# Nine small edits to a one-core transformer-block kernel: the order of the down projection, four squares moved to another engine, a smaller sum of squares, later loads, one split matmul, and two banks for the last rows

## The chip, the cores and the metric

The kernel runs on one core of a Trainium2 chip. The metric is the device time of one execution in microseconds (us). Matmuls run on TensorE (PE, its weight loads PEld), element-wise work on VectorE (DVE), ScalarE (ACT) and GpSimd (POOL). SyncE (SP) issues most of the DMA transfers; POOL issues a few.

## The reference

One layer, 512 tokens, model width 1024, all in float32. Three sub-layers, each normalised before and after and added to the stream `x`:

```python
# 1. token mixer: heads 0-7 forgetting attention ("fox"), heads 8-15 chunked attention with relative bias
proj = rms_norm(x, g_mix_pre) @ w_in
o_fox, o_chk = fox_attention(...), chunked_rel_attention(...)           # 512 x 512 each
y = concat(rms_norm(o_fox, g_fox_out), rms_norm(o_chk, g_chunk_out)) @ w_out
x = x + rms_norm(y, g_mix_post)
# 2. cross-attention, 4 heads of 256, into 256 memory rows
q, (k, v) = rms_norm(x, g_mem_pre) @ w_mem_q, split(rms_norm(mem, g_mem_kv) @ w_mem_kv)
x = x + rms_norm(softmax(q k^T / 16) v @ w_mem_o, g_mem_post)
# 3. feed-forward, hidden width 2816
g, u = split(rms_norm(x, g_ffn_pre) @ w_gate_up)
x = x + rms_norm((silu(g) * u) @ w_down, g_ffn_post)
```

## The kernel before

**Precision.** Every product of two float32 matrices is three matmuls in a reduced type: each operand is split in a high part and a low rest, and `mm3` (line 142) adds high by high (L143), high by low (L144) and low by high (L146). With `parts=IN_STEP` (L140) it issues the last of the three as two matmuls of 128 columns instead of one of 256.

**Weights** come in 512 KB pieces. For the mixer and the cross-attention, `load_unit` (L106) loads a piece into `raw` (three buffers, issued by SP), ACT casts the high half (L125), DVE subtracts for the low half (L126). For the feed-forward network, pieces `fraw` go through a ring of slots: ACT casts `ring_hi` (L920), DVE subtracts `ring_lo` (L921). `take` (L1020) hands out slots in the order of a list of items and refills each slot that is free again.

**Mixer.** While `x` and the V weights stream in at the start, the squares of `x` are added up in `xs` (two blocks of 512 columns); `feature_rstd` (L251, called at L341) sums them over the features by fp32 matmuls with one column, four row tiles by two blocks. `head` (L523) works through four query tiles: scores, exponential, normalisation `p*rc` on DVE (L548), transposes on PE (L551), casts of the transposed `p` (ACT L553, DVE L554), products with V into bank `ps_o` (L560), ACT copy `ot` (L568) and a DVE add that gives the output pair `o` (L569). After each pair, `pair_out` (L571) makes its high and low halves (ACT, DVE) and has POOL square it (L577 the first of a group, L579 the others) and add the squares up (L580). `mem_norm` (L592) normalises the memory `mm` on DVE (L595) and splits it in `mT` (ACT L598, DVE L599).

**Order of instructions.** A tile scheduler sets the order on each engine from the order of the code and from priorities (`later`, L96), so that an instruction more or less in the attention moves its neighbours on other engines too.

**Mixer's end.** The first half of the output projection (fox heads) is mixed into the chunk heads. Then `kT` is made from `mT` and the K weights in four steps `c` (L694 is ACT's cast, L695 DVE's rest), POOL issues four loads `xo` of rows of `x` (L700), and the second half of the output projection follows, whose rows are finished with `xo` at L723.

**Feed-forward network.** The hidden width is cut in eleven blocks `u`. In most, gate and up are made by a seven-product scheme (`seven` L1108, products of 256 columns by `product` L1086); `IN_STEP` is asked for at `u` 1, 2, 4, 6 and 8 (L1186). The down projection (L1236 to the end) runs over the two halves of the output columns:

```python
SEVEN = (4, 5, 6, 7, 8)
DOWN = ((0, 1, 2, 3, 4, 5, 6, 7, 8, 9, 10), (0, 4, 5, 6, 7, 8, 1, 2, 3, 9, 10))
for half, tail in enumerate((2, 3)):
    body = DOWN[half][: FB // 2 - tail]
```

Blocks in `SEVEN` are done by seven products of 128 rows by 256 columns (`seven_products` L1276, using banks `p1 p5 p7 p6`), the others by 24 matmuls of 512 columns (`down` L1257: four row tiles, two k, three terms). After the last seven, `gather` (L1287) puts the seven-product sums together into `yd` on ACT and DVE. The last `tail` blocks are done row tile by row tile, and each row tile is finished (DVE add L1339/1348, ACT square, DVE gain L1341/1350) while the next one is multiplied. In half 1 the last row tile's tail is done in two halves of 256 columns, `left` and `right`, of one bank; then come the add, the square, the sum of squares, its power -0.5 on POOL (L1352), two DVE operations (L1355) and two output DMAs. `mm` (L1245) splits the third matmul of a product where `cuts` holds a column. While block 4 runs in half 0, the operands of blocks 9 and 8 are prepared (`late` L1226, `late_seven` L1207).

## Time and profile before

| what | before |
|---|---|
| median of 3 runs (lowest to highest) | 773.94 us (773.6 to 775.16) |
| the profiled execution | 775.14 us, its span 773.4 us |
| granted TensorE clock | 0.999 of full speed |
| PE busy | 758.1 us (98%), 5019 matmuls |
| DVE busy | 598.6 us (77%) |
| ACT busy | 429.3 us (56%) |
| POOL busy | 61.7 us (8%) |

The profiled execution took 1.2 us more than the median of the runs; 1.74 us of its time lie outside its span. Busy times are sums over the span. On PE a row's duration is longer than its distance to the next row, because matmuls overlap: the cost of a matmul on a full PE is the distance of starts. A bracket such as "[0.64 <-DVE p L548]" says that the engine stood idle 0.64 us before the row, and which instruction's end released it.

### The profile page before, as it was taken

How to read it: one execution, taken by the hardware profiler on the slowest of the kernel's cores; microseconds unless marked ns; L12 is line 12 of the kernel's file. 1: busy time of each engine (PE TensorE's matmuls, PEld its weight loads, DVE VectorE, ACT ScalarE, POOL GpSimd, SP SyncE). 2: the span in 40 equal slices, each digit the busy share in tenths (PEclk: the TensorE clock that was granted, in tenths of full speed). 3: DMA queues.
4: the chain of work that ended last, by engine and by line, in shares of the span. 5: the costliest groups of instructions: out<-in, count | busy, mean ns of one | idle time of the engine just before them, and what ended most of it. 6: DMA issues, size and time to landing. Idle time of an engine off the chain costs nothing.

```text
span 773.4 us, 12904 instructions
## 1 busy us (share of the span) xinstructions
PE 758.1 (98%) x5019; PEld 679.0 (88%) x5019; DVE 598.6 (77%) x1094; ACT 429.3 (56%) x782; POOL 61.7 (8%) x101
## 2 busy tenths in 40 slices
PE   9999999999999999999999999999999999999996
PEld 9977888887788888877778899999999999898985
DVE  8568889789886588554662779999899999987735
ACT  7468889667875457444563625554444445553421
POOL 1001132110321101000001100000000000000001
PEclk9999999999999999999999999999999999999999
DMA  7422113422323725321351202332433332333212
GB/s 272 119 76 81 28 56 87 132 82 63 109 75 105 274 85 189 120 70 57 109 158 33 82 29 82 111 110 82 138 110 109 109 108 87 107 106 113 102 62 109
DMA packets 60748, 80.05 MB, mean 104 GB/s; under 512 B 2704, under 2 KB 43664, under 8 KB 60688
## 3 DMA queue, kind: packets, MB, share of 16 engines
q1 hardware_dynamic: 59264, 74.49, 30.1%
q0 software_dynamic: 1280, 4.72, 1.8%
q8 instruction: 39, 0.64, 0.3%
q14 instruction: 21, 0.17, 0.1%
q10 hardware_dynamic: 144, 0.02, 0.0%
HBM read 77.13 MB, written 2.10 MB: 102 GB/s over the span
## 4 chain that ended last, share of the span: by engine, by line
PE 86%; ACT 6%; DVE 4%; issue 2%; DMA 2%; POOL 0%; DVEq 0%; POOLq 0%; ACTq 0%
PE ps_a L144 13%; PE ps_a L146 13%; PE ps_a L143 13%; PE ps_a L1090 3%; PE ps_a L1093 3%; PE ps_a L1091 3%; PE ps_s L1090 3%; PE ps_s L1091 3%; PE ps_s L1093 3%; PE ps_s L143 2%; PE ps_s L144 2%; PE ps_s L146 2%; PE ps_t L551 2%; DMA raw<-in_dram 2%; PE ps_o L560 2%
## 5 line engine op out<-in xcount | busy, mean ns | idle before, releaser
L920 ACT CAST ring_hi<-fraw 128x1024 fp32r<-128x1024 f32 (+1 forms) x62 | 57.3, 932 | 58.4 <-DVE fraw L999 17.5
L126 DVE TENSOR_TENSOR lo<-raw,hi 128x1024 fp32r<-128x1024 f32 x56 | 68.2, 1224 | 22.0 <-ACT hi L125 21.7
L921 DVE TENSOR_TENSOR ring_lo<-fraw,ring_hi 128x1024 fp32r<-128x1024 f32 (+1 forms) x62 | 66.4, 1074 | 17.2 <-ACT ring_hi L920 17.0
L146 PE MATMUL ps_a<-hTh,lo 128*128 128x512 f32 x192 | 76.7, 399 | 0.0
L144 PE MATMUL ps_a<-hTl,hi 128*128 128x512 f32 x192 | 75.9, 396 | 0.0
L143 PE MATMUL ps_a<-hTh,hi 128*128 128x512 f32 x192 | 75.9, 395 | 0.0
L125 ACT CAST hi<-raw 128x1024 fp32r<-128x1024 f32 x56 | 57.8, 1048 | 26.2 <-PE ps_a L144 18.3
L920 ACT CAST ring_hi<-sums 128x1024 fp32r<-128x1024 f32 x34 | 35.7, 1049 | 33.7 <-PE ps_t L1091 10.1
L921 DVE TENSOR_TENSOR ring_lo<-sums,ring_hi 128x1024 fp32r<-128x1024 f32 x34 | 41.4, 1218 | 2.1 <-ACT ring_hi L920 2.1
L144 PEld LDWEIGHTS ps_a<-hTl,hi 128*128 128x128 f32 x192 | 36.1, 188 | 6.4
L146 PEld LDWEIGHTS ps_a<-hTh,lo 128*128 128x128 f32 x192 | 36.1, 188 | 6.3
L143 PEld LDWEIGHTS ps_a<-hTh,hi 128*128 128x128 f32 x192 | 36.2, 188 | 5.7
L546 ACT ACTIVATE p<-p,nm 128x128 f32<-128x128 f32 (+1 forms) x64 | 36.1, 564 | 8.1 <-DVE nm L536 7.2
L1090 PE MATMUL ps_a<-b,ring_hi 128*128 128x256 f32 x140 | 39.1, 279 | 0.0
L1093 PE MATMUL ps_a<-b,ring_lo 128*128 128x256 f32 (+1 forms) x145 | 39.0, 275 | 0.0
L1091 PE MATMUL ps_a<-b,ring_hi 128*128 128x256 f32 x140 | 38.7, 277 | 0.0
L1090 PE MATMUL ps_s<-b,ring_hi 128*128 128x256 f32 x128 | 35.4, 276 | 0.0
L1091 PE MATMUL ps_s<-b,ring_hi 128*128 128x256 f32 x128 | 35.4, 276 | 0.0
L1093 PE MATMUL ps_s<-b,ring_lo 128*128 128x256 f32 x128 | 35.4, 276 | 0.0
L553 ACT CAST pth<-ps_t 128x128 fp32r<-128x128 f32 (+1 forms) x64 | 27.0, 425 | 14.5 <-PE ps_t L551 13.7
L554 DVE TENSOR_TENSOR ptl<-ps_t,pth 128x128 fp32r<-128x128 f32 (+1 forms) x64 | 30.7, 486 | 5.0 <-ACT pth L553 3.8
L551 PE MATMUL ps_t<-ident,p 128*128 128x128 f32 x160 | 28.1, 275 | 1.1 <-DVE p L548 0.8
(543 smaller groups left out, 2630.9 us busy)
## 6 DMA issues: line engine op xcount, KB each, us to landing
raw<-in_dram SPq DMA_DIRECT2D x64, 512.0 KB, 3.7
fraw<-in_dram SPq DMA_DIRECT2D x62, 512.0 KB, 3.5
cb<-in_dram SPq DMA_DIRECT2D x8, 256.0 KB, 2.9
xo<-in_dram POOLq DMA_DIRECT2D x4, 512.0 KB, 5.3
out_dram<-yd SPq DMA_DIRECT2D x8, 256.0 KB, 2.0
rawv<-in_dram SPq DMA_DIRECT2D x3, 520.0 KB, 6.6
xt<-in_dram SPq DMA_DIRECT2D x3, 512.0 KB, 6.7
gb<-in_dram POOLq DMA_DIRECT2D x3, 512.0 KB, 4.7
```

The costliest lines, as they stand in the source:

```text
L125: act.copy(hi[:, j : j + n, :], raw)
L126: dve.tensor_tensor(out=lo[:, j : j + n, :], in0=raw, in1=f32(hi[:, j : j + n, :]), op=ALU.subtract)
L143: pe.matmul(dst, sh, mh, start=first, stop=False)
L144: pe.matmul(dst, sh, ml, start=False, stop=False)
L146: pe.matmul(dst[:, to], sl, mh[:, to], start=False, stop=last)
L546: act.activation(p[:, :n], p[:, :n], AF.Exp, bias=nm, scale=-1.0, accum_out=sm)
L551: pe.transpose(tp[:, k * P : (k + 1) * P], p[:, k * P : (k + 1) * P], ident)
L920: act.copy(h2, v)
L921: dve.tensor_tensor(out=l2, in0=v, in1=f32(h2), op=ALU.subtract)
L1090: pe.matmul(dst, w[0][:, k, :], b[:, 0, k, :], start=first and k == 0, stop=False)
L1091: pe.matmul(dst, w[0][:, k, :], b[:, 1, k, :], start=False, stop=False)
L1093: pe.matmul(dst[:, to], w[1][:, k, :], b[:, 0, k, to], start=False, stop=last and k == 3)
```

## The change

Nine edits, in the order of the program (line numbers of the kernel before, with the changed kernel's in brackets where they differ):

1. The two blocks of `xs` are added by DVE (new L338), and `feature_rstd` sums one block.
2. `pair_out` gets `side`: squares of the chunk heads (side 1) are done by ACT instead of POOL; POOL still adds them up.
3. The four `xo` loads are issued after step 2 of the `kT` loop instead of after the loop, each buffer being written first by a POOL copy of a column of `kT` (new L705), which the load must then wait for.
4. Block 10 of gate and up asks for `IN_STEP` too.
5. In half 0 of the down projection block 10 stands between sevens 7 and 8, and the tail is one block, not two.
6. In half 0 the last seven gets a cut of a matmul like the first.
7. The preparation of blocks 9 and 8 is written after seven 6 instead of after seven 4.
8. The last row tile of half 1 is finished from two banks of its own, half by half: the sum of the body is added to `yd` before, each half is added, squared and multiplied by the gain alone.
9. The end of a row tile is a function, `finish_rows`.

```diff
             if k == 6:
                 add_squares(0, 4)
+                dve.tensor_tensor(out=xs[:, 0, :], in0=xs[:, 0, :], in1=xs[:, 1, :], op=ALU.add)
...
-                    rcol = feature_rstd(xs, range(2), NT, "rx")
+                    rcol = feature_rstd(xs, range(1), NT, "rx")
...
-        def pair_out(o, gc, oh, ol, sq, first, total):
+        def pair_out(o, gc, oh, ol, sq, first, total, side):
...
-            if first:
-                pool.tensor_tensor(out=sq, in0=o, in1=o, op=ALU.mult)
+            dst = sq if first else o
+            if side:
+                act.activation(dst, o, AF.Square)
             else:
-                pool.tensor_tensor(out=o, in0=o, in1=o, op=ALU.mult)
+                pool.tensor_tensor(out=dst, in0=o, in1=o, op=ALU.mult)
+            if not first:
                 pool.tensor_tensor(out=total, in0=sq, in1=o, op=ALU.add)
...
-        for t in range(NT):
-            nc.gpsimd.dma_start(xo[t], x[t * P : (t + 1) * P, :])
+                if c == 2:
+
+                    for t in range(NT):
+                        pool.tensor_copy(xo[t][:, :1], f32(kT[:, 0, 4, t : t + 1]))
+                        nc.gpsimd.dma_start(xo[t], x[t * P : (t + 1) * P, :])
...
-        DOWN = ((0, 1, 2, 3, 4, 5, 6, 7, 8, 9, 10), (0, 4, 5, 6, 7, 8, 1, 2, 3, 9, 10))
+        DOWN = ((0, 1, 2, 3, 4, 5, 6, 7, 10, 8, 9), (0, 4, 5, 6, 7, 8, 1, 2, 3, 9, 10))
...
-            parts = IN_STEP if u in (1, 2, 4, 6, 8) else WHOLE
+            parts = IN_STEP if u in (1, 2, 4, 6, 8, 10) else WHOLE
...
-        for half, tail in enumerate((2, 3)):
+        for half, tail in enumerate((1, 3)):
...
-                    if half == 0 and i == SEVEN[0]:
+                    if half == 0 and i in (SEVEN[0], SEVEN[-1]):
                         cuts.append(P)
                     seven_products(i, i == SEVEN[-1])
-                    if half == 0 and i == SEVEN[0]:
+                    if half == 0 and i == SEVEN[2]:
...
             for t in range(NT):
-                parts = (left, right) if half and t == NT - 1 else (slice(0, 512),)
                 yt = yd[:, t, cs]
...
+                if half and t == NT - 1:
+
+                    ss1, r = small(2, "fss2"), small(1, "frs")
+                    dve.tensor_tensor(out=yt, in0=accs[t], in1=yt, op=ALU.add)
+                    for n, (to, b) in enumerate(((left, bank("a")), (right, bank("a")))):
+                        for j, w in enumerate(ends):
+                            down(t, DOWN[half][FB // 2 - tail + j], w, j == tail - 1, (to,), b)
+                        dve.tensor_tensor(out=yt[:, to], in0=b[:, to], in1=yt[:, to], op=ALU.add)
+                        act.activation(junk3[:, to], yt[:, to], AF.Square, scale=1.0 / 32.0, accum_out=ss1[:, n : n + 1])
+                        if n == 0:
+                            dve.tensor_tensor(out=r, in0=ss1[:, :1], in1=ss0[:, t : t + 1], op=ALU.add)
+                        dve.tensor_tensor(out=gained[:, to], in0=yt[:, to], in1=gb3[:, c0 + to.start : c0 + to.stop], op=ALU.mult)
+                    dve.tensor_tensor(out=r, in0=ss1[:, 1:], in1=r, op=ALU.add)
+                    finish_rows(t, r)
+                    continue
```

**Order on ACT, at the end of the chunk heads.** `ps_o` is the bank of the last head's product with V, `ot` its copy, `mT` the memory's high half, `hi` the weights, `mix` the output projection's first half. Before:

```order
L553 CAST pth_413<-ps_t_2808 128x3x128
L553 CAST pth_413<-ps_t_2825 128x4x128
L656 ACTIVATE mix<-ps_a_2953,rsg_1877 128x512
L598 CAST mT<-mm 128x2048
L568 COPY ot_2841<-ps_o_2832 64x512
L125 CAST hi_3007<-raw_0_3009 128x1024
L125 CAST hi_3007<-raw_4_3013 128x1024
L656 ACTIVATE mix<-ps_a_2967,rsg_1877 128x512
L572 ACTIVATE oh<-o_2660,gn 128x512
```

And with the change:

```order
L554 CAST pth_410<-ps_t_2805 128x3x128
L554 CAST pth_410<-ps_t_2822 128x4x128
L659 ACTIVATE mix<-ps_a_2950,rsg_1874 128x512
L569 COPY ot_2838<-ps_o_2829 64x512
L601 CAST mT<-mm 128x2048
L573 ACTIVATE oh<-o_2657,gn 128x512
L125 CAST hi_3004<-raw_0_3006 128x1024
L125 CAST hi_3004<-raw_4_3010 128x1024
L659 ACTIVATE mix<-ps_a_2964,rsg_1874 128x512
L579 ACTIVATE o_2657<-o_2657 128x512
```

The copy `ot` now stands ahead of the cast of `mT`, the copy `oh` ahead of the two casts `hi`, and the new square (L579) comes last. On PE, 10 matmuls of the output projection now stand between the last product with V and the first matmul that reads `mT`, where there were 7.

**Order on POOL, from the second chunk pair to the loads of `xo`.** Before:

```order
L580 TENSOR_TENSOR sq_1869<-sq_1869,o_2046 128x512
L619 TENSOR_TENSOR msq<-msq 128x512 x3
L579 TENSOR_TENSOR o_2493<-o_2493 128x512
L151 TENSOR_TENSOR rm_2747<-rm_2747,mhalf 128x2
L580 TENSOR_TENSOR sq_1869<-sq_1869,o_2493 128x512
L579 TENSOR_TENSOR o_2660<-o_2660 128x512
L580 TENSOR_TENSOR sq_1869<-sq_1869,o_2660 128x512
L679 DMA gb<-in_dram 128x1024
L151 TENSOR_TENSOR rsg_2988<-rsg_2988,mhalf 128x4
L700 DMA xo_3003<-in_dram 128x1024
```

And with the change:

```order
L583 TENSOR_TENSOR sq_1866<-sq_1866,o_2043 128x512
L622 TENSOR_TENSOR msq<-msq 128x512 x3
L583 TENSOR_TENSOR sq_1866<-sq_1866,o_2490 128x512
L151 TENSOR_TENSOR rm_2744<-rm_2744,mhalf 128x2
L583 TENSOR_TENSOR sq_1866<-sq_1866,o_2657 128x512
L682 DMA gb<-in_dram 128x1024
L151 TENSOR_TENSOR rsg_2985<-rsg_2985,mhalf 128x4
L705 COPY xo_3000<-kT 128x1
L705 COPY xo_3001<-kT 128x1
L705 COPY xo_3002<-kT 128x1
L705 COPY xo_3003<-kT 128x1
L706 DMA xo_3000<-in_dram 128x1024
```

The squares have left POOL, the sums of them have stayed, and ahead of the first load of `xo` stand four copies that read `kT`.

## Rows read from the trace of the kernel before

**Rows 1.** The page: busy time of each engine, its share of the span and its instructions.

```profile
PE 758.1 (98%) x5019; PEld 679.0 (88%) x5019; DVE 598.6 (77%) x1094; ACT 429.3 (56%) x782; POOL 61.7 (8%) x101
```

**Rows 2.** Two windows of the span, the end of the chunk heads and the down projection: start and end, length, then busy us (and instructions) of PE, PEld, DVE, ACT and POOL, the granted PE clock, the busy share of the DMA engines and GB/s.

```profile
200.00:238.00 38.00, 37.74 (x202) 30.33 (x201) 31.64 (x90) 30.87 (x65) 7.89 (x6) 1.00 0.17 56
...
653.00:766.00 113.00, 113.00 (x727) 102.40 (x725) 85.73 (x137) 44.30 (x66) 2.21 (x4) 1.00 0.29 99
```

**Rows 3.** Timeline of the start, PE and DVE: the one-column matmuls of `feature_rstd` (L255), the next matmul, and the DVE operation behind them. Columns: start, duration, engine, line, operation, output<-input, shapes, count.

```profile
26.39 1.84 PE L255 MATMUL ps_t<-ones,xs 128*128 128x1 f32 x16
28.09 0.37 PE L143 MATMUL ps_s<-vhi,hTh 128*128 128x264 f32 x1
...
28.27 0.16 DVE L150 TENSOR_SCALAR rx<-ps_t 128x4 f32<-128x4 f32 x1 [5.85 <-PE ps_t L255]
```

**Rows 4.** Timeline of POOL, DVE and PE at two squares of the chunk pairs.

```profile
178.41 1.04 POOL L577 TENSOR_TENSOR sq<-o 128x512 f32<-128x512 f32 x1 [4.55 <-DVE o L569]
178.71 1.03 DVE L548 TENSOR_SCALAR p<-p,rc 128x512 f32<-128x512 f32 x1
179.35 0.40 PE L144 MATMUL ps_a<-hTl,hi 128*128 128x512 f32 x1
179.88 0.30 PE L551 MATMUL ps_t<-ident,p 128*128 128x128 f32 x1
...
197.47 1.03 POOL L579 TENSOR_TENSOR o<-o 128x512 f32<-128x512 f32 x1 [2.48 <-DVE rc L547]
197.69 0.89 DVE L548 TENSOR_SCALAR p<-p,rc 128x128 f32<-128x128 f32 x1
198.64 0.33 PE L551 MATMUL ps_t<-ident,p 128*128 128x128 f32 x1 [0.64 <-DVE p L548]
```

**Rows 5.** The lines L548, L617 (ACT's squares of the memory, 512 columns) and L580 (POOL's sums of squares) as groups: for the first two count, then least, median and longest ns; for the third count, busy us, mean ns and idle before.

```profile
L548 DVE TENSOR_SCALAR p<-p,rc x64: 270/410/1026, 63.5 to 231.7; 128x128 f32<-128x128 f32 x16, 128x256 f32<-128x256 f32 x16, 128x384 f32<-128x384 f32 x16, 128x512 f32<-128x512 f32 x16
...
L617 ACT ACTIVATE msq<-mm x4: 614/632/634, 205.0 to 210.3; 128x512 f32<-128x512 f32 x4
...
L580 POOL TENSOR_TENSOR sq<-sq,o 128x512 f32<-128x512 f32 x6 | 8.8, 1473 | 0.4
```

**Rows 6.** Timeline of ACT, DVE and PE where the products of `mT` begin.

```profile
236.19 1.91 ACT L598 CAST mT<-mm 128x2048 fp32r<-128x2048 f32 x1 [0.73 <-DVE mm L595]
238.12 0.58 ACT L568 COPY ot<-ps_o 64x512 f32<-64x512 f32 x1
238.13 2.29 DVE L599 TENSOR_TENSOR mT<-mm,mT 128x2048 fp32r<-128x2048 f32 x1 [1.97 <-ACT mT L598]
238.64 0.28 PE L143 MATMUL ps_a<-mT,hi 128*128 128x256 f32 x1
240.48 0.38 PE L144 MATMUL ps_a<-mT,hi 128*128 128x256 f32 x1 [0.16 <-DVE mT L599]
```

**Rows 7.** Where the second half of the output projection begins: POOL's issues of `xo`, one load `raw` as it stands in the chain of waits that ended last (start, length), an ACT cast of `kT`, two matmuls of PE, the landing times of the loads `xo`, and the first use of one.

```profile
253.50 2.15 POOL L700 DMA_DIRECT2D xo<-in_dram  x4
255.20 7.86 DMA raw<-in_dram
258.66 0.58 ACT L694 CAST kT<-ps_a 128x512 fp32r<-128x512 f32 x1
264.45 0.39 PE L143 MATMUL ps_a<-hi,oh 128*128 128x512 f32 x1
265.45 0.50 PE L144 MATMUL ps_a<-lo,oh 128*128 128x512 f32 x1 [0.61 <-DVE lo L126]
...
DMA to landing us min/median/max: 4.0/5.3/7.6
...
282.72 1.28 DVE L723 SCALAR_TENSOR_TENSOR mix<-mix,prs,xo 128x1024 f32<-128x1024 f32 x1
```

**Rows 8.** The page: the loads `raw` by count, size and median us from issue to landing.

```profile
raw<-in_dram SPq DMA_DIRECT2D x64, 512.0 KB, 3.7
```

**Rows 9.** Timeline of PE: the first matmul of block 10 of gate and up, the first matmul of the down projection; then three rows there, of which the first two have a split matmul between them (L1255) and the last two eleven distances.

```profile
632.64 0.28 PE L1090 MATMUL ps_a<-b,ring_hi 128*128 128x256 f32 x1
652.42 0.39 PE L143 MATMUL ps_a<-ring_hi,g 128*128 128x512 f32 x1
674.45 0.33 PE L1255 MATMUL ps_s<-ring_hi,latex 128*128 128x128 f32 x2
674.79 0.28 PE L144 MATMUL ps_s<-ring_lo,latex 128*128 128x256 f32 x1
676.04 0.28 PE L143 MATMUL ps_a<-ring_hi,latex 128*128 128x256 f32 x1
```

**Rows 10.** Groups of DVE's work by line, from 698 to 716 us, where the tail of half 0 runs: count, busy us, mean ns, idle before.

```profile
L1341 DVE TENSOR_TENSOR yd<-yd,gb 128x512 f32<-128x512 f32 x4 | 2.8, 693 | 1.8 <-ACT spare L1340 1.7
L921 DVE TENSOR_TENSOR ring_lo<-fraw,ring_hi 128x1024 fp32r<-128x1024 f32 x2 | 2.5, 1226 | 1.8 <-ACT ring_hi L920 1.8
L1339 DVE TENSOR_TENSOR yd<-ps_a,yd 128x512 f32<-128x512 f32 x3 | 2.1, 685 | 0.0
```

**Rows 11.** Timeline of the end: DVE and the last matmul.

```profile
764.95 0.75 DVE L1355 SCALAR_TENSOR_TENSOR yd<-spare,frs,mix 128x512 f32<-128x512 f32 x1
765.85 0.28 PE L146 MATMUL ps_t<-ring_hi,g 128*128 128x256 f32 x1
766.17 0.76 DVE L1348 TENSOR_TENSOR yd<-ps_t,yd 128x256 f32<-128x256 f32 x2 [0.47 <-PE ps_t L146]
```

More of the change, by code (lines that the diff above doesn't have):

```diff
@@ L643, in hybrid_block_kernel @@
                         o, (G_FOX, G_CHK)[side] + pr, oh[:, 4 * side + pr, :], ol[:, 4 * side + pr, :],
-                        sqs[side], n % 2 == 0 and b == 0, sqs[side],
+                        sqs[side], n % 2 == 0 and b == 0, sqs[side], side,
                     )
@@ L1234, in hybrid_block_kernel, with finish_rows @@
         yd = big.tile([P, NT, D], F32, tag="sB", name="yd")
+        def finish_rows(t, r):
+            pool.tensor_tensor(out=r, in0=r, in1=mhalf[:, :1], op=ALU.pow)
+            for hf in range(2):
+                c2 = slice(hf * 512, (hf + 1) * 512)
+                dve.scalar_tensor_tensor(
+                    out=yd[:, t, c2], in0=(yd[:, t, c2], gained)[hf], scalar=r, in1=xr[:, t, c2],
+                    op0=ALU.mult, op1=ALU.add,
+                )
+                nc.sync.dma_start(out[t * P : (t + 1) * P, c2], yd[:, t, c2])
         ss0 = small(NT, "fss0")
-        for half, tail in enumerate((2, 3)):
+        for half, tail in enumerate((1, 3)):
             c0 = half * 512
@@ L1255, in mm, with down @@
                     pe.matmul(dst[:, part], lhs[1], rhs[0][:, part], start=False, stop=end)
-            def down(t, i, w, end=False, parts=(slice(0, 512),)):
+            def down(t, i, w, end=False, parts=(slice(0, 512),), dst=None):
                 ts = slice(t * P, (t + 1) * P)
+                dst = accs[t] if dst is None else dst
                 for to in parts:
@@ L1262, in down @@
                         mm(
-                            accs[t], to, (gh[k][:, ts], gl[k][:, ts]), (w[0][:, j, to], w[1][:, j, to]),
+                            dst, to, (gh[k][:, ts], gl[k][:, ts]), (w[0][:, j, to], w[1][:, j, to]),
                             end and j == 1 and to is parts[-1],
@@ L1329, in hybrid_block_kernel @@
                         cuts.append(384)
-                    down(t, i, w)
+                    down(t, i, w, half == 1 and t == NT - 1 and i == body[-1])
             ends = take(tail)
             for t in range(NT):
-                parts = (left, right) if half and t == NT - 1 else (slice(0, 512),)
                 yt = yd[:, t, cs]
-                for to in parts:
-                    for j, w in enumerate(ends):
-                        down(t, DOWN[half][FB // 2 - tail + j], w, j == tail - 1 and to is parts[-1], (to,))
+                if half and t == NT - 1:
[12 more added lines that the diff above has]
+                    continue
+                for j, w in enumerate(ends):
+                    down(t, DOWN[half][FB // 2 - tail + j], w, j == tail - 1)
                 if half == 0:
@@ L1346, in hybrid_block_kernel @@
                     r = small(1, "frs")
-                    for to in parts:
-                        dve.tensor_tensor(out=yt[:, to], in0=accs[t][:, to], in1=yt[:, to], op=ALU.add)
+                    dve.tensor_tensor(out=yt, in0=accs[t], in1=yt, op=ALU.add)
                     act.activation(junk3, yt, AF.Square, scale=1.0 / 32.0, accum_out=ss1)
@@ L1351, in hybrid_block_kernel @@
                     dve.tensor_tensor(out=r, in0=ss1, in1=ss0[:, t : t + 1], op=ALU.add)
-                    pool.tensor_tensor(out=r, in0=r, in1=mhalf[:, :1], op=ALU.pow)
-                    for hf in range(2):
-                        c2 = slice(hf * 512, (hf + 1) * 512)
-                        dve.scalar_tensor_tensor(
-                            out=yd[:, t, c2], in0=(yd[:, t, c2], gained)[hf], scalar=r, in1=xr[:, t, c2],
-                            op0=ALU.mult, op1=ALU.add,
-                        )
-                        nc.sync.dma_start(out[t * P : (t + 1) * P, c2], yd[:, t, c2])
+                    finish_rows(t, r)
 _WEIGHTS = ["w_out", "w_mem_q", "w_mem_kv", "w_mem_o", "w_gate_up", "w_down"]
```

## The prediction

> **What bounds the kernel now.** I read the busy times first: PE works 758.1 of 773.4 us, DVE 77%, ACT 56%, POOL 8% [rows 1]. So only two things shorten this program: PE work that goes away, and PE's idle or stretched stretches, which make some 15 us in all. Next the windows: in the down projection, where the change's largest edit lies, PE is busy 113.00 of 113 us, so there is nothing to gain there, while at the end of the chunk heads DVE and ACT are busy for 31.6 and 30.9 of 38 us and POOL for 7.9 [rows 2]. A gain is therefore to be looked for in small places, each read from its own timeline: the start [rows 3], the squares [rows 4, 5], the entry into the memory products [rows 6], the second half of the output projection [rows 7, 8], and the spacing of PE's matmuls [rows 9]. The distance of starts is a matmul's cost: eleven distances of 256 columns take 676.04 - 674.79 = 1.25 us [rows 9], 0.1136 each, and 512 columns cost twice that, 0.23.
>
> **The change part by part.**
>
> *Start (edit 1).* Four row tiles by two blocks, in fp32, show as 16 matmuls of one column; they take 28.09 - 26.39 = 1.70 us, 0.106 each [rows 3]. With one block eight of them go: **-0.85**. The added DVE operation reads 512 columns, about 0.7 us by the DVE adds of that size [rows 10]. DVE stands idle for 5.85 us before the result of these matmuls is read [rows 3], so it is hidden; uncovered, it would cost its 0.7.
>
> *Squares (edit 2).* DVE's normalisation of `p` took 1.03 us on 512 columns while POOL's square ran beside it, and 0.89 on 128 columns beside another, where the least is 0.27 [rows 4, 5]. PE paid: the transposes of the first start at 179.88, though the matmul before them (179.35) left the engine free at about 179.58, so 0.30; the second waited 0.64 [rows 4]. Together 0.94, the most that the four squares' move can give back here. But POOL's three additions behind these squares stay, at 1.47 us each [rows 5]: POOL's exposed time in the chunk heads falls from 4 x 1.03 + 3 x 1.47 = 8.5 to 4.4 us, about half. If collisions fall by chance, the gain is half of 0.94, if only these two places count, all of it. I take **-0.7**, between them. ACT gets 4 x 0.63 = 2.5 us more [rows 5], where it has 7 of 38 us free [rows 2]; half of one square late on the way to a transposed `p`, +0.3, is the other end.
> In the row the DVE operation ends at 179.74, about 0.29 after POOL's, and both ran in SBUF: one stood still until the other was through. The Trainium skill, "SBUF — State Buffer", section "Who interferes with whom", says that a DVE `tensor_scalar` in a two-port mode and a GpSimd operation hold their shared ports exclusively for a whole instruction, and that ACT never waits. The trace agrees with the first part (0.89 for 0.27). By that rule the additions that stay block DVE just as the squares did, and the gain here would be nothing (a rival, below).
>
> *Order at the memory products (follows from 2).* On ACT the copy `ot` now stands ahead of the cast of `mT`, and must wait for the last head's product with V; behind that product PE has ten matmuls (10 x 0.23 = 2.3 us) before it first reads `mT`, at a time X. So the last product starts at about X - 2.4 and ends by X - 2.1. Then ACT copies (0.58) to X - 1.5 and casts (1.91) to X + 0.4, and DVE makes the rest (2.29) to X + 2.75 [rows 6]. The first matmul that reads the rest stands third there. Before, it came 240.48 - 238.64 = 1.84 us behind X [rows 6]; now at about 2.8: **+0.96**. From 0 (if ACT's new wait overlaps another) to +1.4.
>
> *Loads of `xo` (edit 3).* In the second half of the output projection PE waits 0.61 us for a low half, and its two starts lie 1.00 us apart instead of 0.23 [rows 7]: 0.77 lost. The cause is four steps back: one load `raw` took 7.86 us, from 255.20 on, against a median of 3.7 [rows 7, 8], because it was issued while the four `xo` loads (253.50 to 255.65) were in flight. Now POOL's copies wait for the cast of `kT`'s step 2, which ended at 258.66 + 0.58 [rows 7], so the loads start some 5 us later, when this `raw` has landed: at its median it would be there by 258.9, at 6 us by 261.2, both ahead of need. **-0.77**, and the later issue is covered: landing within 7.6 us, by 260 + 7.6 = 268, and even 4 us later, they are wanted at 282.72 [rows 7]. Without that cover a late `xo` would hold one DVE operation, not PE at once. Lower end 0, if another load meets them in the same way.
>
> *`IN_STEP` at block 10 (edit 4).* Block 10 has two sevens of 84 matmuls, from 632.64 to 652.42: 19.78 / 168 = 0.1177 us each. Behind a split in the down projection the distance is 0.1136, as above. If the split brings the pace back, 168 x 0.0041 = -0.69; the split's own price is 0.34 us for what else takes two distances [rows 9], at most +0.11. Net **-0.6**; ends -0.7 and +0.13.
>
> *Down projection (edits 5, 6, 7).* No PE work is removed, and PE has no idle time here [rows 2]; one cut adds 0.11, about what a restored pace gives. **0**, from -0.3 to +0.15. What gets shorter is a cover: behind `gather` two blocks stood (48 x 0.23 = 11 us), now one (5.4). DVE must do four additions of the gather, four adds and four gains at about 0.69 each, and the ring's fills at 1.23 [rows 10], by when half 1 needs its banks and weights. The gather frees the banks 4 x 0.69 = 2.8 us after the last seven, well ahead of the 5.4. The fills stand in a queue that has slack of several blocks, so I cost it at nothing, and keep it as a rival.
>
> *End (edits 8, 9).* PE's last matmul starts at 765.85; DVE is busy with the third row tile until 765.70 (764.95 + 0.75) [rows 11]. The left half can thus start only just before the right one ends, and the chain after it (add, square, sum, power, two gains, output) is shorter by half a square (0.3) but has one more small add and one more ACT operation: **0**, from -0.4 to +0.3.
>
> Sum: -0.85 - 0.7 + 0.96 - 0.77 - 0.6 = **-2.0**. The profiled execution of 775.14 would become 773.1; it lies 1.2 over the median of the runs, so against 773.94 the forecast is **771.9**. A change of 0.2% (1.55 us) is about what a measurement of this kernel can tell from no change.
>
> **Rivals.**
>
> *No delay at the memory products.* If `ot` finds ACT waiting for `mm` anyway, or if the products with V move up, +0.96 falls away: 773.94 - 2.96 = 771.0. For it: ACT stood 0.73 us idle before this cast [rows 6]. Against: the chain above holds whatever X is.
>
> *The collisions only move.* The three additions that stay on POOL meet other DVE operations and give the 0.7 back: 772.6. For it: they are longer (1.47) than the squares. It decides where an addition now starts within the 0.3 to 1.0 us that a normalisation takes. Against: each ran beside DVE before, too. This is the case that the Trainium skill's rule above would lead to.
>
> *The split does nothing (the change doesn't do what it says).* The pace of block 10 stays at 0.1177, and the split costs 0.13 instead of giving 0.6: 772.7. For it: the trace shows no split there.
>
> *The down projection starves: slower.* One mechanism: DVE's list behind the last seven of half 0 is four gather adds, four adds, four gains and the next fill, 12 x 0.69 + 1.23 = 9.5 us [rows 10], where one block of PE work is 5.4. If half 1's next weights stand behind that list, PE waits 4.1 us, and the time is 773.94 - 2.0 + 4.1 = 776.0. It decides from the point at which that fill ends later than the blocks already in the ring are used up; with four slots, up to three blocks (16 us) are there, which speaks against it.
>
> **How the numbers follow.** Forecast 0.46, no delay 0.14, collisions move 0.18, split without effect 0.11, starved 0.11. The forecast's own bounds (some 0.8 either way) put 0.04 of it within 0.2% (above 772.39); of the moved collisions 0.12 lie there, of the useless split all. Faster by over 0.2%: 0.42 + 0.14 + 0.06 = 0.62. Within: 0.04 + 0.12 + 0.11 = 0.27. Slower: 0.11. The range goes from 770.4 (no delay at the memory products, and 0.6 of the lower bounds) to 774.6: collisions moved and the split useless, 773.94 - 2.0 + 0.7 + 0.73 = 773.4, with the dear ends of the memory products (+0.44) and of the `xo` loads (+0.77). It leaves out the starvation, 0.11, and some 0.04 below.
>
> **What would show it.** Each step has its place in the changed profile: the one-column matmuls take 0.85 us; no DVE normalisation over 0.6 us in the chunk heads; the first matmul that reads the low half of `mT` comes 2.8 us behind the first that reads the high half; no wait of PE for a low half in the second output projection, and the `raw` load there lands in under 5 us; distances of 0.1136 in block 10; PE busy without a gap in the down projection; DVE's last operations at the same distance from PE's last matmul. The forecast is wrong if PE shows a wait of over 1 us behind the last seven of half 0, or if L548 still shows 0.9 to 1.0 us beside POOL's additions.

## The result, and the profile after

The changed kernel is slower: 777.18 us against 774.52 (medians of 7 runs each), ratio 1.0032, 95% interval 1.0022 to 1.0041. A second set of runs of the same two kernels (below, "the changed kernel again") gave 1.0015 (1.0006 to 1.0024, 12 and 35 runs). The forecast was 771.9, faster by 2.0; the profiled execution took 776.9, its span is 775.1 against 773.4, and its mean granted clock 0.995 against 0.999. The kernel before was profiled in an execution 0.6 above its median, the changed one in an execution 0.3 below its own, so the traces show 1.76 of the 2.66 us between the medians.

PE works through the same products in the same stages, so the two traces can be laid side by side at points of PE's work. The table gives the start of a point in the kernel before, and how much later (+) or earlier (-) each trace is there; behind it, in brackets, what it lost (+) or gained (-) since the point above. The labels are those of the experiments below.

```
point of PE's work             before   changed        again          e1             e10            e2             e5
first product behind the sum    28.09   -1.03          -0.88          -1.37          -0.03          -1.11          -1.17
last matmul ahead of mT        238.42   +0.73 (+1.76)  +0.72 (+1.60)  -1.38 (0.0)    +1.58 (+1.61)  -0.92 (+0.19)  +0.52 (+1.69)
last matmul that reads mT      262.95   +3.19 (+2.46)  +3.37 (+2.65)  -1.36 (0.0)    +2.99 (+1.41)  +1.72 (+2.64)  +1.54 (+1.02)
ninth matmul behind it         265.78   +2.32 (-0.87)  +2.50 (-0.87)  -2.24 (-0.88)  +2.99 (0.0)    +0.84 (-0.88)  +0.66 (-0.88)
first of the down projection   652.42   +1.26 (-1.06)  +2.25 (-0.25)  -1.84 (+0.40)  +2.22 (-0.77)  +1.10 (+0.26)  -0.54 (-1.20)
last matmul                    765.85   +1.81 (+0.55)  +2.40 (+0.15)  -1.32 (+0.52)  +3.11 (+0.89)  +1.63 (+0.53)  -0.53 (0.0)
end of the span                773.37   +1.76          +2.36          -1.07          +3.09          +1.57          -0.60
```

Two stretches lose 4.2 us between them, the chunk heads up to 238 us and the products that read `mT`; the start and the second output projection gain 1.9, where 1.6 was forecast. The windows of the changed kernel (start:end and length, then PE, PEld, DVE, ACT and POOL busy, clock, DMA share, GB/s) say the same:

```profile
200.00:238.00 38.00, 36.18 (x194) 29.58 (x193) 31.32 (x89) 29.22 (x66) 7.05 (x5) 1.00 0.17 56
238.00:266.00 28.00, 26.06 (x205) 25.07 (x204) 16.27 (x16) 12.96 (x15) 6.25 (x11) 0.94 0.45 150
653.00:766.00 113.00, 112.94 (x723) 102.04 (x722) 86.37 (x139) 45.09 (x67) 2.16 (x4) 1.00 0.28 98
```

Against [rows 2], PE is idle for 1.82 us of the 38 where it was for 0.26, and in the next stretch the granted clock is 0.94. ACT is not busier in the first of them (29.22 against 30.87), and POOL hardly less (7.05 against 7.89).

The start does what was forecast. Eight one-column matmuls take 0.81 us (27.06 - 26.25), where [rows 3] has 1.70 for sixteen.

```profile
26.25 0.95 PE L255 MATMUL ps_t<-ones,xs 128*128 128x1 f32 x8
27.06 0.37 PE L143 MATMUL ps_s<-vhi,hTh 128*128 128x264 f32 x1
```

In the chunk heads, the timeline of POOL, DVE and PE at the places that answer to [rows 4]:

```profile
198.00 1.27 POOL L583 TENSOR_TENSOR sq<-sq,o 128x512 f32<-128x512 f32 x1 [2.59 <-ACT o L579]
198.03 1.39 DVE L549 TENSOR_SCALAR p<-p,rc 128x256 f32<-128x256 f32 x1
199.48 0.44 PE L552 MATMUL ps_t<-ident,p 128*128 128x128 f32 x2 [0.69 <-DVE p L549]
...
213.17 1.27 POOL L622 TENSOR_TENSOR msq<-msq 128x512 f32<-128x512 f32 x1 [2.01 <-ACT msq L620]
213.33 1.39 DVE L549 TENSOR_SCALAR p<-p,rc 128x512 f32<-128x512 f32 x1
213.56 0.41 PE L533 MATMUL ps_s<-T,Q 128*128 128x384 f32 x1 [0.70 <-DVE nm L537]
214.87 0.63 PE L552 MATMUL ps_t<-ident,p 128*128 128x128 f32 x4 [0.72 <-DVE rc L548]
...
224.37 1.42 DVE L126 TENSOR_TENSOR lo<-raw,hi 128x1024 fp32r<-128x1024 f32 x1
224.66 1.76 POOL L151 TENSOR_TENSOR rm<-rm,mhalf 128x2 f32<-128x2 f32 x1
226.48 0.49 PE L264 MATMUL ps_t<-ident,rm 128*128 128x128 f32 x2 [0.27 <-POOL rm L151]
```

The squares are gone from POOL, and the sums that stayed do what the squares did: the normalisation of 256 columns takes 1.39 us (0.35 in the median) beside an addition that began 0.03 before it, and 512 columns take 1.39 (0.48) beside POOL's sum of the memory's squares. Where the reader should look is the pair of starts: in both, POOL's is the earlier one, and DVE's operation ends only 0.15 and 0.28 after POOL's. In the last three rows DVE's subtraction is the earlier one, and POOL's power of two columns ends only after it. The kernel before had a stop by an addition too, in rows that the prediction did not look at (128 columns take 0.28 in the median):

```profile
224.48 2.31 POOL L580 TENSOR_TENSOR sq<-sq,o 128x512 f32<-128x512 f32 x1
225.97 0.91 DVE L548 TENSOR_SCALAR p<-p,rc 128x128 f32<-128x128 f32 x1
```

At the memory products, ACT, DVE and PE, against [rows 6]:

```profile
237.35 0.58 ACT L569 COPY ot<-ps_o 64x512 f32<-64x512 f32 x1 [1.15 <-PE ps_o L561]
237.95 1.91 ACT L601 CAST mT<-mm 128x2048 fp32r<-128x2048 f32 x1
239.77 0.71 ACT L573 ACTIVATE oh<-o,gn 128x512 fp32r<-128x512 f32 x1
239.90 2.29 DVE L602 TENSOR_TENSOR mT<-mm,mT 128x2048 fp32r<-128x2048 f32 x1 [1.24 <-ACT mT L601]
239.92 0.38 PE L143 MATMUL ps_a<-mT,hi 128*128 128x256 f32 x1 [0.38 <-ACT mT L601]
240.39 1.98 ACT L125 CAST hi<-raw 128x1024 fp32r<-128x1024 f32 x2
241.47 0.38 PE L143 MATMUL ps_a<-mT,hi 128*128 128x256 f32 x1 [1.17 <-ACT hi L125]
242.24 0.58 PE L144 MATMUL ps_a<-mT,hi 128*128 128x256 f32 x1 [0.40 <-DVE mT L602]
```

Three waits in a row, 0.38 + 1.17 + 0.40, where before there were 1.02 and 0.16. And then, by windows of one microsecond of the same trace:

```profile
241.00:242.00 1.00, 0.38 (x1) 0.19 (x1) 1.00 (x1) 1.00 (x2) 0.00 (x0) 0.96 0.00 0
242.00:243.00 1.00, 0.76 (x3) 0.76 (x4) 1.00 (x3) 1.00 (x3) 0.00 (x0) 0.50 0.00 0
243.00:244.00 1.00, 1.00 (x7) 1.00 (x6) 1.00 (x2) 0.52 (x1) 0.34 (x1) 0.50 0.00 0
244.00:245.00 1.00, 1.00 (x7) 1.00 (x7) 1.00 (x1) 0.00 (x0) 1.00 (x1) 0.50 0.00 0
245.00:246.00 1.00, 1.00 (x9) 1.00 (x9) 1.00 (x1) 0.00 (x0) 0.66 (x2) 0.83 0.90 294
```

The granted clock is at half, 1.2 GHz, from 241.9 to 245.3, behind 239.5 to 241.9 in which PE mostly waited. PE reads as busy there, but issues 7 matmuls in a microsecond where e5 below issues 11 or 12. That is the part of the loss which no wait shows.

### The profile page after: what moved, and what is told of

It is laid out like the page before. It is cut to its first block, busy times and chain, and to the rows that moved or that the text cites. A ratio compares the mean times of both kernels' runs of the same rounds, so it can differ in the third digit from the quotient of the medians.

```text
span 775.1 us, 12902 instructions
## 1 busy us (share of the span) xinstructions
PE 758.5 (98%) x5013; PEld 680.0 (88%) x5013; DVE 601.7 (78%) x1098; ACT 431.4 (56%) x788; POOL 57.8 (7%) x101
## 4 chain that ended last, share of the span: by engine, by line
PE 78%; DVE 9%; ACT 7%; issue 3%; DMA 2%; POOL 1%; DVEq 0%; POOLq 0%; ACTq 0%; SPq 0%
PE ps_a L144 12%; PE ps_a L146 12%; PE ps_a L143 12%; PE ps_a L1099 3%; PE ps_a L1096 3%; PE ps_a L1097 3%; PE ps_s L1096 2%; PE ps_s L1097 2%; PE ps_s L1099 2%; PE ps_s L143 2%; PE ps_s L144 2%; PE ps_s L146 2%; PE ps_t L552 2%; PE ps_o L561 2%; DVE ring_lo L927 2%
```

## The experiments

All were timed in turn with the kernel before on the same chip; ratios are to it. e1 to e4 ran on one chip, the second run of the changed kernel and e5 to e7 on another, e8 to the end on a third.

**e1: the squares back on POOL.**

```diff
-            if side:
-                act.activation(dst, o, AF.Square)
-            else:
-                pool.tensor_tensor(out=dst, in0=o, in1=o, op=ALU.mult)
+            pool.tensor_tensor(out=dst, in0=o, in1=o, op=ALU.mult)
```

> The changed kernel with the four squares of the chunk heads back on POOL; all else as changed. The order on every engine through the attention is then that of the kernel before. Theory: the move of the squares, with the new order that it brings and the fall of the clock behind it, is what made the changed kernel slower; between 167 and 257 us of the kernel before it lost 2.3 + 1.9 = 4.2 us in the trace, so about 777.2 - 4.2 = 773.0, ratio to the kernel before 0.998 (1.002 at most 0.999). The clock stays at 1.00 around 242 us. Rival: the loss at the memory products comes from the other edits (the later loads, the start), and only the 2.3 come back: 774.9, ratio 1.000, and the clock falls to 0.50 for 3 us as in the changed kernel.

Measured 0.9979 (0.9970 to 0.9988), the clock at 1.00 throughout PE's work. The theory holds: the table's column e1 loses nothing between 28 and 263 us, and both stretches are as in the kernel before. The edit to the squares, with the order that it brings, turned a gain of 0.2% into a loss.

**e2: short additions on POOL.**

```diff
-                pool.tensor_tensor(out=total, in0=sq, in1=o, op=ALU.add)
+                w = 64 if side else SEQ
+                pool.tensor_tensor(out=total[:, :w], in0=sq[:, :w], in1=o[:, :w], op=ALU.add)
```

> The changed kernel, but POOL's three additions of the chunk heads' squares take 64 columns of the 512 (the other columns are left out of the sum). The order on every engine stays. Theory: an addition that stays on POOL stops DVE's normalisation beside it as the squares did (1.39 us for 256 columns at 198.03 beside an addition from 198.00 on, and PE waited 0.69 behind it); with short additions that wait goes: -0.7 (0.5 to 1.0), about 776.5, ratio to the kernel before 1.0025. Rival: DVE and PE are late because ACT's squares stand ahead of its exponentials, and the additions don't matter: no difference, 777.2, ratio 1.0033.

Measured 1.0014 (1.0005 to 1.0022). The same place in its trace:

```profile
197.75 0.31 POOL L584 TENSOR_TENSOR sq<-sq,o 128x64 f32<-128x64 f32 x1 [2.59 <-ACT o L579]
197.79 0.43 DVE L549 TENSOR_SCALAR p<-p,rc 128x256 f32<-128x256 f32 x1
198.41 0.38 PE L552 MATMUL ps_t<-ident,p 128*128 128x128 f32 x2
```

With the addition cut to 0.31 us the normalisation takes 0.43, and PE's wait of 0.69 is gone. So is the wait for `rm`: its power, no longer held up by an addition in POOL's queue, starts ahead of DVE's subtraction and takes 0.72. The chunk heads lose 0.19 instead of 1.76: the additions cost 1.57 in the trace, twice the 0.7 that was expected. The rival (ACT's squares in the way) falls. The 0.19 is a balance, though. The collision with the sum of the memory's squares, which this edit leaves as it is, still takes 1.39, with PE's waits of 0.68 and 0.72 around it, while the waits behind the squares of [rows 4] are gone. The stretch behind loses 2.64 as in the changed kernel, clock at 0.50 included, so the two losses are separate. The time alone would not show all this: 1.0014 lies beside the changed kernel's 1.0015 and below its 1.0032, and neither was timed beside it.

```profile
212.22 1.39 DVE L549 TENSOR_SCALAR p<-p,rc 128x512 f32<-128x512 f32 x1
213.75 0.63 PE L552 MATMUL ps_t<-ident,p 128*128 128x128 f32 x4 [0.72 <-DVE rc L548]
```

**e3: PE kept busy at the memory products.**

```diff
             for c in range(4):
                 hi, lo = unit()
                 acc = bank("a")
+                if c == 0:
+                    for _ in range(12):
+                        pe.matmul(acc[:, 256:], hi[:, 0, :P], mT[:, 0, 0, :], start=True, stop=True)
```

> The changed kernel with 12 more matmuls of 256 columns between the first and the second matmul that read mT, where PE waits 1.17 us for ACT; their result is overwritten. Theory: the loss behind the waits for mT is the clock, 0.50 of full speed from 242.0 to 245.3 us, which follows PE's idle time there; with PE busy the clock stays at 1.00 and 3.3 x 0.5 = 1.6 us come back, less 0.2 for the added work that does not fit the wait: -1.4, about 775.8, ratio to the kernel before 1.0015. Rival: the clock falls for another reason, or the waits themselves are the loss: 777.2 to 777.5, ratio 1.0033 to 1.0037, with the clock at 0.50 as before.

Measured 1.0031 (1.0016 to 1.0046), but in two groups: six runs from 774.7 to 777.0 and six from 778.9 to 781.1. The profiled execution belongs to the first: clock 1.00, span 773.6, 1.5 below the changed kernel's, as the theory has it. What makes the second group slow is open. It is not the clock: its six runs have a mean of 0.997 to 0.999. The edit had also moved a cast of weights ahead of a `kT` cast on ACT, but two runs of e8, which leaves that order alone, lie some 4 us above its others too. Inconclusive as a time.

**e4: the old down projection.**

```diff
-        DOWN = ((0, 1, 2, 3, 4, 5, 6, 7, 10, 8, 9), ...
+        DOWN = ((0, 1, 2, 3, 4, 5, 6, 7, 8, 9, 10), ...
...
-        for half, tail in enumerate((1, 3)):
+        for half, tail in enumerate((2, 3)):
...
-                    if half == 0 and i in (SEVEN[0], SEVEN[-1]):
+                    if half == 0 and i == SEVEN[0]:
...
-                    if half == 0 and i == SEVEN[2]:
+                    if half == 0 and i == SEVEN[0]:
```

> The changed kernel with the down projection of half 0 as in the kernel before: its order of blocks, a tail of two blocks, one cut, and the operands of blocks 9 and 8 prepared after seven 4. Theory: these edits cost 0.4 at the second part of seven 7 (ring fills late behind the preparations) and 0.15 more up to the tail, 0.55 in all: 776.6, ratio to the kernel before 1.0026. Rival: what the trace shows there is a shift of one execution, and the edits are worth nothing or gain 0.1: 777.2, ratio 1.0033 to 1.0035.

Measured 1.0041 (1.0029 to 1.0053, six runs): the theory wanted a faster kernel, and this one is slower if anything. The theory falls. PE waits twice there, 0.63 and 0.64 us, for low halves of ring weights.

**The changed kernel again,** with no edit.

> The changed kernel once more, unaltered, to stand on the same chip as the three others and to give a second trace. All theories: ratio to the kernel before 1.003 (1.002 to 1.004), the clock at 0.50 around 242 us, and the two normalisations beside POOL's sums at 1.2 to 1.4 us again. Which of the waits near 632 us and 690 us differ from the first trace shows what belongs to the execution and not to the kernel.

Measured 1.0015 (1.0006 to 1.0024), below the range expected. The two collisions return to the hundredth (1.39 and 1.39 us), and so do the losses of both stretches. What differs is the wait in block 9 of gate and up: none in the first trace, 0.96 us in the second (ACT had waited 1.62 and 1.13 us for ring loads ahead of it), none in e5, and between 0.2 and 1.4 in the others. That belongs to the execution. So does the clock: in this set the mean clock was 0.997 or 0.998 in seven runs, 774.99 to 776.74 us, and 0.995 or 0.996 in five, 776.28 to 778.33. The first seven have a median of 775.17, 0.2 above the kernel before beside them (774.99), the other five one of 777.5. In the first set six runs of seven had 0.995 or 0.996, which goes some way to explain why its ratio is the larger one. Over both sets it is 11 of 19 runs; of the 90 runs of the kernel before that were timed beside the experiments none lies below 0.997.

**e5: two fp32 matmuls as filling, without the moved cast.**

```diff
+                if c == 0:
+                    for _ in range(2):
+                        pe.matmul(acc[:, 256:], f32(hi[:, 0, :P]), f32(mT[:, 0, 0, :]), start=True, stop=True)
```

> The changed kernel with two fp32 matmuls of 256 columns (about 0.9 us together) ahead of the first matmul that reads both mT and the second piece of weights; the order on ACT, DVE and POOL stays that of the changed kernel (the twelve short matmuls had also moved a cast on ACT). Theory: the clock stays at 1.00 around 242 us, and some 1.4 us come back: ratio 1.0013 (1.0003 to 1.0023), in all runs alike, so that the split of the first try in two groups of runs came from the moved cast. Rival: PE's waits set the loss and the clock falls as before: 1.003 to 1.0035.

Measured 1.0006 (0.9998 to 1.0015), against 1.0015 for the changed kernel beside it. PE's rows and the clock:

```profile
239.69 1.13 PE L691 MATMUL ps_a<-mT,hi 128*128 128x256 f32 x4 [0.36 <-ACT mT L601]
241.24 0.39 PE L143 MATMUL ps_a<-mT,hi 128*128 128x256 f32 x1 [0.30 <-ACT hi L125]
242.02 0.39 PE L144 MATMUL ps_a<-mT,hi 128*128 128x256 f32 x1 [0.39 <-DVE mT L602]
```

```profile
242.00:243.00 1.00, 0.98 (x8) 0.98 (x9) 1.00 (x2) 1.00 (x3) 0.00 (x0) 1.00 0.00 0
243.00:244.00 1.00, 1.00 (x11) 1.00 (x11) 1.00 (x2) 0.29 (x1) 0.57 (x1) 1.00 0.00 0
244.00:245.00 1.00, 1.00 (x12) 1.00 (x11) 1.00 (x1) 0.00 (x0) 1.00 (x2) 1.00 0.10 22
```

PE does 0.8 us of useless work (239.69 to 240.47) and is 1.4 to 1.6 us faster through the stretch (+1.02 instead of +2.46 and +2.65), since the clock stays at 1.00. The runs' gain, 0.0009, is half of that; five of the twelve runs of the changed kernel beside it have the lower mean clock, and none of the 35 runs of e3, e5 and e8, the kernels with filling, has.

**e6: squares on POOL, and the old down projection** (the edits of e1 and e4 together):

```diff
+            pool.tensor_tensor(out=dst, in0=o, in1=o, op=ALU.mult)
...
+        DOWN = ((0, 1, 2, 3, 4, 5, 6, 7, 8, 9, 10), ...
+        for half, tail in enumerate((2, 3)):
```

> The squares back on POOL and the down projection of half 0 as in the kernel before: the start, the later loads, the split at block 10 and the end are what is left of the change. Theory: DVE is full from 653 to 690 us with the old order (36.55 of 37 us before), so that what PE gains ahead of it turns into waits for low halves of weights, as with the old down projection in the changed kernel (0.80 and 0.81 in its trace); the new order is what lets the gains through: ratio 0.9995 (0.999 to 1.000), against 0.998 with the new order. Rival: the new order is worth nothing, and the waits belonged to one execution: 0.998.

Measured 0.9984 (0.9975 to 0.9993). The rival's 0.998 lies inside this interval and the theory's 0.9995 outside it, though the theory's lower end, 0.999, lies inside: the time does not settle it. The trace loses 0.99 us from the first matmul of the down projection to the last, 0.7 of it at one place:

```profile
688.93 0.38 PE L144 MATMUL ps_s<-ring_lo,latelo 128*128 128x256 f32 x1 [0.48 <-DVE ring_lo L924]
```

**e7: e1 without the split at block 10.**

```diff
-            parts = IN_STEP if u in (1, 2, 4, 6, 8, 10) else WHOLE
+            parts = IN_STEP if u in (1, 2, 4, 6, 8) else WHOLE
```

> The squares back on POOL, the rest as changed, but without the split at block 10. Theory: the split gives block 10 its pace back, 168 matmuls by 0.004 less 0.1, so without it 0.4 to 0.6 us more than with it: ratio 0.9985 (0.998 to 0.999), and distances of 0.1177 through block 10 wherever PE waited in block 9. Rival: the wait in block 9 is what costs, and the pace gained is lost again in the down projection, where DVE sets the pace: 0.998, no difference.

Measured 0.9975 (0.9967 to 0.9984): no gain from the split; the rival holds as a time. It has the lowest ratio here, though the interval overlaps those of e1 and e6, and it beats both kernels.

**e8: e2 and e5 together:**

```diff
+                        pe.matmul(acc[:, 256:], f32(hi[:, 0, :P]), f32(mT[:, 0, 0, :]), start=True, stop=True)
...
+                pool.tensor_tensor(out=total[:, :w], in0=sq[:, :w], in1=o[:, :w], op=ALU.add)
```

> The changed kernel with both cures at once: two fp32 matmuls fill PE's wait for the second piece of weights, and POOL's three additions take 64 columns of 512 (the rest is left out of the sum). The order on ACT, DVE and POOL stays that of the changed kernel. Theory: the additions' stops of DVE (1.4 us by the chunk heads' end) and the fall of the clock (1.3 to 1.5) are two separate losses, and both go: about 2.8 us less than the changed kernel's 1.0015 to 1.003, so 0.9985 (0.9975 to 0.9995). Rival: the two are one loss (PE late, whatever the cause), and the second cure adds nothing to the first: 1.0005.

Measured 0.9994 (0.9981 to 1.0007), between the two theories, with two of its twelve runs at 778.6 and the others from 773.55 to 775.31. In its trace both cures add up: +0.16 in the chunk heads and +1.03 behind, and the span is 772.8.

**e9: the start and the later loads alone** (edits 1 and 3 on the kernel before):

```diff
+                dve.tensor_tensor(out=xs[:, 0, :], in0=xs[:, 0, :], in1=xs[:, 1, :], op=ALU.add)
+                    rcol = feature_rstd(xs, range(1), NT, "rx")
...
+                if c == 2:
+                    for t in range(NT):
+                        pool.tensor_copy(xo[t][:, :1], f32(kT[:, 0, 4, t : t + 1]))
+                        nc.gpsimd.dma_start(xo[t], x[t * P : (t + 1) * P, :])
```

> The kernel before with two edits alone: the halved sum of squares at the start and the later loads of xo. Theory: these two are all that gains, 1.1 and 0.8 us in every trace that has them, and the orders of the down projection, the split at block 10 and the end are worth nothing in sum: 1.9 us less, ratio 0.9976 (0.997 to 0.9985). Rival: the other edits carry a part: 0.9985 to 0.999 here, and the whole change without the squares below it.

Measured 0.9993 (0.9984 to 1.0002), a smaller gain than either expected, though the rival's 0.9985 to 0.999 lies inside the interval. In the trace the two bring 1.04 and 0.88, and 1.13 of it is lost again in the down projection with its old order:

```profile
689.84 0.38 PE L144 MATMUL ps_s<-ring_lo,latelo 128*128 128x256 f32 x1 [0.64 <-DVE ring_lo L924]
```

**e10: the squares on ACT alone** (edit 2 on the kernel before):

```diff
+            if side:
+                act.activation(dst, o, AF.Square)
+            else:
+                pool.tensor_tensor(out=dst, in0=o, in1=o, op=ALU.mult)
```

> The kernel before with one edit alone: the four squares of the chunk heads on ACT. Theory: this edit alone makes the loss, 1.7 us in the chunk heads and 2.4 at the memory products, of which 1.3 to 1.5 by the clock at 0.50: 4.1 us more, ratio 1.0053 (1.003 to 1.0065). Rival: the loss at the memory products needs the other edits (the start, or the later loads), and 1.7 us are left: 1.002.

Measured 1.0049 (1.0037 to 1.0061, five runs), near the theory's 1.0053. Here is PE at the memory products, and the clock:

```profile
240.77 0.38 PE L143 MATMUL ps_a<-mT,hi 128*128 128x256 f32 x1 [0.38 <-ACT mT L600]
242.32 0.38 PE L143 MATMUL ps_a<-mT,hi 128*128 128x256 f32 x1 [1.17 <-ACT hi L125]
243.10 0.39 PE L144 MATMUL ps_a<-mT,hi 128*128 128x256 f32 x1 [0.39 <-DVE mT L601]
```

```profile
242.00:243.00 1.00, 0.38 (x1) 0.19 (x1) 1.00 (x2) 1.00 (x2) 0.00 (x0) 1.00 0.00 0
243.00:244.00 1.00, 0.90 (x7) 0.91 (x8) 1.00 (x3) 1.00 (x3) 0.00 (x0) 1.00 0.00 0
```

The same three waits to a hundredth, and in this execution the clock did not fall (two of the five runs have a mean clock of 0.994 and 0.995). Up to the third of these matmuls the waits cost 1.04; a slower spacing behind them, 0.118 us instead of 0.1136 until 253.7, makes it 1.41. The changed kernel's two traces have 1.03 and 1.02 at the third matmul, and no slower spacing once the clock is back. So the fall costs them 1.4 and 1.6, as e5 says, or 1.0 to 1.2 more than this execution lost.

**e1 again, beside e9.**

> The changed kernel with the squares back on POOL once more, to stand on the same chip as the start and the later loads alone. Theory: 0.9978 (0.997 to 0.9987), the same as those two alone. Rival: the split at block 10 and the new order of the down projection add to them: 0.001 or more below the two alone.

Measured 0.9983 (0.9973 to 0.9993), 0.001 below e9; the intervals overlap, so the times leave it open. The traces favour the rival, and name the edit: from its first matmul to its last the new order lost 0.0 to 0.55 us in nine traces, the old one 0.89 to 1.69 in the four that are not the kernel before itself (e4, e6, e9, e10).

## Why the prediction was wrong, step by step

- **Start, -0.85:** right. -0.88 to -1.42 in the traces with it; DVE's added operation took 0.69 us, and DVE still stood idle for 3.87 us before the sum was read.
- **Squares, -0.7 (ends -0.94 and +0.3): wrong, and the step that failed.** I credited the two collisions of [rows 4] as gone and expected the remaining additions to cost half as often. In fact the collisions had successors: from 160 us on, what DVE's normalisations took over the median of their size sums to 2.02 us before and 1.90 after. My own sign of being wrong, a normalisation of 0.9 to 1.0 us beside POOL's additions, came true at 1.39. The stretch lost 1.6 to 1.8, and 1.57 of it went when the additions were made short. The rival "the collisions only move" had the mechanism and 0.18 of the chance, but its price, 0 instead of -0.7, was still too kind: PE waits 0.69, 0.72 and 0.27 us behind the new stops, and 0.13 and 0.64 behind the old squares. My upper end, +0.3, was drawn from ACT's load, which at +0.19 in e2 matters little, and not from a new collision. By the rule that I weighed there, this step would have been priced at nothing. That rule, of the Trainium skill, "SBUF — State Buffer", section "Who interferes with whom", says besides that issue order decides who stops. The trace agrees with the lock (1.39 us for what takes 0.43 beside a short addition) and with the order (the power of `rm` takes 1.76 us behind a subtraction that began before it, and 0.72 where it begins first). A shift of the order on ACT and POOL is thus a new draw of collisions.
- **Order at the memory products, +0.96 (0 to +1.4):** right in mechanism and sign: the third matmul starts 2.32 us behind the first (1.84 before), and the first itself waits 0.38, so that the third is 1.02 to 1.04 later than before in the changed kernel's traces and in e10. By the last of these matmuls it is 1.41 in e10, where the clock did not fall, which is my upper end: for some 11 us behind the waits their distance stays about 0.004 us longer, as in block 10 before. The wait of 1.17 for the weights' high half, which the copy `oh` now delays, was not in my chain; the chain hides it, since the third matmul waits for the rest of `mT` in any case.
- **The clock:** not foreseen at all, +1.4 and +1.6 in the changed kernel's two traces behind the waits themselves. The granted clock was 1.00 through PE's work before, and I did not ask what a longer wait would do to it. By the mean clocks of the runs it fell in about 11 of 19. The Trainium skill, "TensorE: Matmul & The Clock Gate", section "Part 1: The HAM clock gate", says that idle time throttles the engine and that the point of change varies from run to run; e10 beside the changed kernel agrees: equal waits, 1.00 in the one, 0.50 in the other.
- **Loads of `xo`, -0.77:** right, -0.87 or -0.88 in every trace that has the edit. In the changed kernel's trace they were issued from 263.6 on, later than my 260, and landed in 10.3 us at most, by 275.5, ahead of their first use at 285.0. The `raw` load that had taken 7.86 took 3.49; a later one that met them took 10.69, and PE did not wait for it.
- **Split at block 10, -0.6:** the pace came back, but not by the split alone, and the time did not. In the first trace block 10 took 653.68 - 634.52 = 19.16 us instead of 19.78, and 19.2 in all ten traces that have the split; yet of the four without it only two have the slow pace (19.78 before, 19.79 in e7), and e9 and e10 take 19.04, less than with the split. I took -0.6 from one draw. e7 without the split is as fast as e1 with it; the wait in block 9, 0 to 1.4 us by the execution, is larger than what is left.
- **Down projection, 0:** 0.55 and 0.15 lost against the kernel before in this place, but one trace of it is a poor comparison. Four other traces with the old order lose 0.9 to 1.7 there, nine with the new one half a microsecond or nothing. The reason is argued, not shown: the matmul that waits for DVE in e6, e9 and e10 starts 58.3 to 58.6 us behind the first matmul of block 10, and 58.15 in the kernel before, where block 10 itself took 0.6 to 0.75 longer and PE hardly waited. What a faster block 10 gains, the old order gives back here. So the edit seems to work, and my sum had no row for it. The starved rival did not occur: PE was busy 112.94 of 113 us.
- **End, 0:** right; 7.47 us from the last matmul to the end, 7.52 before (7.76 in e1 and 7.75 in e7).

So the sum of -2.0 became +1.8 in the trace: +2.5 from the squares, +1.5 from the memory products and the clock, +0.55 from the down projection, and -0.7 from the start, `xo` and block 10, which gave more than forecast. The forecast of "faster" had 0.62 of the chance on terms that I had worked out one by one, and one edit reordered a stage in which DVE and ACT were busy for four fifths of the time. What stays open: the second group of runs in e3 and the two such runs in e8; why the runs with the lower clock are 2.3 us slower in the median and not 1.4 to 1.6; whether it is the squares on ACT or the scheduler's new order that makes the waits at the memory products, since no run has the one without the other; and how much the split and the new order of the down projection are worth alone, below what these runs tell.

## What to carry to other kernels

Moving half of a pair of operations off an engine need not halve its collisions: here the stops summed to 2.02 us before and 1.90 after. List the operations that stay, see which instructions of the other engine they will now start beside, and expect the full price until all of them are gone. Where a scheduler sets the order, cost one edit with its whole reordering, and try it alone. A wait on TensorE, the engine that bounds this kernel, is to be priced twice, once as itself and once with a fall of the clock behind it (1.02 and 1.4 to 1.6 us here), and a stretch that depends on a load (here 0 to 1.4 us) is to be read in more than one trace before a term of half a microsecond is taken from it.

## What was not expected of the hardware

- The collisions of POOL and DVE repeat closely: 1.39 us at both places in the changed kernel's two traces and in e10, 0.89 and 1.03 in all with the squares on POOL.
- The granted clock fell to half for some 3 us in four traces (the changed kernel twice, e2, e4), in or behind the same three waits of 0.38, 1.17 and 0.40 us, and did not in a fifth with the same waits (e10). With PE given work in those waits it did not fall either (e3, e5, e8).
- POOL's power of a 128x2 tile took 1.76 us, and PE waited for it, where a DVE subtraction of two tiles had begun 0.29 us earlier; where the power began first it took 0.71 (before) and 0.72 (e2).
- The spacing of matmuls of 256 columns stayed at 0.118 us instead of 0.1136 behind some waits and not behind others: in block 10 before and in e7, not in e9 and e10; behind the waits for `mT` in e10, not in the changed kernel.
